# A two-layer encoder on one core: the order of layer 1's projections, norm roots in pairs, later transposes, fewer query loads

## Chip, cores and metric

The kernel runs on one core of a Trainium2 chip. The metric is the device time of one execution in microseconds (us), lower is better. Five engines take part, each with an instruction list of its own that it works off in order: TensorE (PE) multiplies matrices, VectorE (DVE), ScalarE (ACT) and GpSimd (POOL) do elementwise work, SyncE (SP) issues the DMA transfers. SBUF is the on-chip memory, PSUM the one that PE writes to.

## Reference

Sequence 2048, width 1024, fp32. Only layer 1 ("odd") is touched by the change:

```python
def odd_layer(x, norm_g, w_in, w_out, qn, kn, ..., subln_g, cos, sin, lambda_init):
    h = rms_norm(x, norm_g)
    q, k, v, gate = jnp.split(h @ w_in, [C_QK, 2 * C_QK, 2 * C_QK + C_W], axis=-1)
    q = rms_norm(q.reshape(b, s, C_HEADS, 2, HEAD_DIM), qn)      # 8 heads, two halves of 64
    k = rms_norm(k.reshape(b, s, C_HEADS, 2, HEAD_DIM), kn)
    q1, q2, k1, k2 = apply_rope(q[..., 0, :]), ...               # rotary by cos, sin
    o = differential_attention(q1, q2, k1, k2, v, lam)           # (softmax1 - lam * softmax2) @ v
    o = rms_norm(o, subln_g) * (1.0 - lambda_init)
    return x + (o.reshape(b, s, C_W) * jax.nn.silu(gate)) @ w_out
```

Layer 0 ("even") has two attention mixers and an output projection of its own, and stands before layer 1.

## The kernel before

**Tiling.** The 2048 tokens are 4 blocks of 512, a block is 4 tiles of 128. Every matrix product is made of three matmuls of 128x512, since each operand is split into a high and a low part (`wH`, `wL` for weights, `hH`, `hL` for the normed input, "hidden"): lines L214 to L216 are wH·hH, wL·hH and wH·hL. An output tile of 128 tokens by 512 columns is 8 × 3 = 24 matmuls in one PSUM place (`p1mm`, four places).

**Stages.** Names begin with the stage: `p0` layer 0's projections, `m` its mixers and its output projection (`mom`), `p1` layer 1's projections, `c` layer 1's attention with gate (`cG`) and output (`com`).

**Layer 1's projections** go over two halves of two blocks each. A half first makes hidden for its two blocks: per tile load x (`p1xt`), square and root of the mean on ACT and DVE, scale (DVE), 8 transposes of 128x128 on PE (`p1trh`), the copies `p1hH` on ACT (L336) and the rests `p1hL` on DVE (L337). Then come six groups of 512 columns: two of queries (tab "q"), two of keys (tab "k"), two of values ("cv"). A group's weights are four chunks of 512 KB (`p1ws`), split by ACT (`p1wH`, L309) and POOL (`p1wL`, L311), with two staging buffers and 28 places for split tiles, 16 to a group. For a query or key tile, ACT squares (`p1sq`, L361), DVE sums over each of 8 heads (`p1qss`, L362), `rstd` computes a root by small instructions on 128x8 (L203 to L208: `p1q8ln`, `p1q8y` on ACT, `p1q8ms`, `p1q8u` twice, `p1q8r` on DVE), DVE multiplies by it (`p1xn`, L366) and forms two half-width rotary products (`p1t`, L373), and POOL multiplies by the cosine (L377) and adds (L378). When a block's four tiles are done, PE transposes them (`p1trq`, L385), ACT copies the high part (`p1eH`), DVE the rest (`p1eL`, L391), and both are stored. `tables()` builds the rotary tables for queries and keys at the start of layer 1's projections, from `cos` and `sin`. A values tile is one ACT copy and a store.

**Ahead.** Beside these groups, the weights of attention (output weights, gate weights) are loaded, split and stored as `wgH`, `wgL` by a generator, one item of four chunks at a time.

**Attention** goes block by block; per head it loads query tiles (`cqd`, `cql`), keys `ck` and values `cv`; PE does scores (`cS`), transposes (`ctr`) and products (`cO`), and between them gate columns (`cG`) from hidden and `cwH`, `cwL` (loaded from `wgH`, `wgL`). For later blocks hidden is loaded again (`p1hH<-hH`).

**What sets the order.** A scheduler places each engine's instructions in a fixed list, from the program and its own timeline; pools are stacked in SBUF, so a tile can have to wait until an older one in the same place is released. All DMAs are issued by SP in order.

Of the kernel before, what the change touches and what calls it, by code (L numbers as in the profile page):

```python
# [10 lines left out]
F32 = mybir.dt.float32  # L11
# [7 lines left out]
P = 128  # L19
S = 2048  # L20
# [12 lines left out]
def f32(ap):  # L33
    return ap.bitcast(F32)
# [52 lines left out]
class Trunk:  # L87
# [136 lines left out]
    def _project(self, es, layer):  # L224
# [39 lines left out]
        def tables():  # L264
            if layer == 0:
                self.parameters(xp.tile([P, D], F32, tag="xt", name=n + "tmp"))
            self.cos = sb.tile([P, S // P, 32], F32, tag="xn", name=n + "cos", bufs=5)
            self.sin = sb.tile([P, S // P, 32], F32, tag="xn", name=n + "sin", bufs=5)
# [3 lines left out]
            with self.tc.issue_after(self.added) if layer else nullcontext():  # L272
                tabs["q"] = self.rope_tables(tb, self.gain[gq], 0.125 if layer else -0.125, n + "tq")
                tabs["k"] = self.rope_tables(tb, self.gain[gk], 1.0, n + "tk")

        if layer == 1:
            tables()
# [78 lines left out]
        def normed(ps, nh, tab, t):  # L356
            wd = nh * HD
            v3 = lambda ap: ap.rearrange("p (h d) -> p h d", d=HD)
            sq = sb.tile([P, 512], F32, tag="sq", name=n + "sq")
            ss = sm.tile([P, 8], F32, tag="qss", name=n + "qss")  # L360
            nc.scalar.activation(sq[:, :wd], ps[:, :wd], AF.Square)  # L361
            nc.vector.tensor_reduce(ss[:, :nh], v3(sq[:, :wd]), AX.X, ALU.add)  # L362
            r = self.rstd(sm, ss[:, :nh], nh, 1.0 / HD, n + f"q{nh}")
            xn = sb.tile([P, 512], F32, tag="xn", name=n + "xn", bufs=5)
            xv = v3(xn[:, :wd])
            nc.vector.tensor_tensor(xv, v3(ps[:, :wd]), r.unsqueeze(2).to_broadcast([P, nh, HD]), ALU.mult)  # L366
            if tab is None:
                return xn
            C, Sn = tabs[tab]
            t2 = sb.tile([P, 512], F32, tag="t2", name=n + "t2")  # L370
            tv = v3(t2[:, :wd])
            for o in (0, 32):
                nc.vector.tensor_tensor(  # L373
                    tv[:, :, o:o + 32], xv[:, :, 32 - o:64 - o],
                    Sn[:, t, o:o + 32].unsqueeze(1).to_broadcast([P, nh, 32]), ALU.mult,
                )
            nc.gpsimd.tensor_tensor(xv, xv, C[:, t, :].unsqueeze(1).to_broadcast([P, nh, HD]), ALU.mult)  # L377
            nc.gpsimd.tensor_tensor(xn[:, :wd], xn[:, :wd], t2[:, :wd], ALU.add)  # L378
            return xn
# [39 lines left out]
        ahead = later()  # L419
        for half in range(2):  # L420
            blocks = (NB - 1 - 2 * half, NB - 2 - 2 * half)
            ready = None
# [7 lines left out]
            if not tabs:  # L430
                tables()
            h.append(hidden(blocks[1], 1))
            self.last_hidden = h[1]
            for gi, (kind, c0, width, o) in enumerate(groups):
                w = ready or weights(c0, width)
                ready = None
                if gi >= self.AHEAD:
                    next(ahead, None)
                for bi, b in enumerate(blocks):
# [21 lines left out]
                    for j in range(NTB):  # L461
# [3 lines left out]
                        if kind == "qk":  # L465
                            xs.append(normed(ps, 8, o["tab"], t))
                        elif kind == "akv":
                            xs.append(normed(ps, 2, o["tab"], t))
# [12 lines left out]
                        else:  # L481
                            vt = gp.tile([P, 512], F32, tag="v", name=n + "v", bufs=3)
# [381 lines left out]
    def _mix1(self, es):  # L864
# [4 lines left out]
        sm = pool("sm", 8)  # L869
        ot = pool("ot", 4)  # L870
        yp = pool("y", 2 * KT)
        vp = pool("v", 4)
        pp = pool("pp", 20)
        kp = pool("kp", 4)
        sb = pool("sb", 2)
# [85 lines left out]
        def values(h, b, res):  # L961
# [3 lines left out]
            for kt in range(nkt):  # L965
                j0 = max(0, kt - b * NTB)
                wd = (NTB - j0) * P
                tp = ptr.tile([P, 512], F32, tag="tr", name=n + "tr")
                kk = (kt % 4) * P
                for j in range(j0, NTB):  # L970
                    nc.tensor.transpose(tp[:, (j - j0) * P:(j - j0 + 1) * P], us[j][kt // 4][:, kk:kk + P], self.ident)  # L971
                T = sb.tile([P, 512], F32, tag="pt", name=n + "pt", bufs=6)
                nc.vector.tensor_copy(T[:, :wd], tp[:, :wd])  # L973
# [297 lines left out]
```

## Time and profile before

| What | Value |
| --- | --- |
| three runs | 2804.6 us median, 2803.25 to 2808.34 |
| profiled execution | 2808.08 us, span 2806.3 us |
| mean granted PE clock of the profiled execution | 0.987 |
| PE busy | 2697.3 us (96%) |
| layer 1's projections | about 1164 to 1763 us of the span |
| attention of layer 1 | about 1763 us to the end |

The profile is of one execution. "Busy" is the time in which an engine executes, "waited" the time in which it stood until another engine or a transfer released it; the granted clock is the share of full speed that TensorE ran at. Times inside the span are us from its start.

### The profile page before, as it was taken

Reading aid. Unit: us, or ns where it says so; the run is one execution under the profiler, and the core shown is the slowest. Engines: PE = TensorE matmul, PEld = TensorE weight load, DVE = VectorE, ACT = ScalarE, POOL = GpSimd, SP = SyncE. Lnnn points to the kernel's source line nnn. Section 1 sums busy time; section 2 is a strip of 40 time slices with the busy share of each in tenths; the row PEclk is TensorE's granted clock in tenths of the full one; section 3 lists DMA queues with packets and bytes.
Section 4 is the critical chain, followed back from the end, with each engine's and each line's share of the span. In section 5 each row is a group of like instructions: output and inputs, shape, how many; then the busy total and the mean of one; then the engine's idle time right before and its main releaser. Section 6 shows DMA issues by size and latency. Waiting matters only on the chain.

```text
span 2806.3 us, 44052 instructions
## 1 busy us (share of the span) xinstructions
PE 2697.3 (96%) x13384; PEld 2169.2 (77%) x13384; DVE 1853.8 (66%) x4616; ACT 1606.4 (57%) x4039; POOL 1462.8 (52%) x1551
## 2 busy tenths in 40 slices
PE   7999999999899999899999999999999999999998
PEld 5888888888788888777788888777676777676776
DVE  7762285346777775598808870569886878777762
ACT  5443543367767675334334331578896787777761
POOL 3541252335545454267745670457676666767661
PEclk9999999999999999999999999999999999999999
DMA  5673343738866764666885444787868666454542
GB/s 174 225 242 140 109 142 122 232 109 239 240 179 191 201 192 132 209 217 207 253 256 192 135 136 142 239 256 219 238 190 230 183 212 200 132 183 144 166 146 83
DMA packets 356093, 521.69 MB, mean 186 GB/s; under 512 B 44816, under 2 KB 139792, under 8 KB 355856
## 3 DMA queue, kind: packets, MB, share of 16 engines
q1 hardware_dynamic: 355856, 518.87, 60.2%
q8 instruction: 107, 1.75, 0.3%
q14 instruction: 130, 1.06, 0.1%
HBM read 361.70 MB, written 157.02 MB: 185 GB/s over the span
## 4 chain that ended last, share of the span: by engine, by line
PE 77%; DVE 9%; DMA 6%; ACT 3%; issue 2%; POOL 2%; SPq 1%; DVEq 0%; ACTq 0%; POOLq 0%
PE cO L975 8%; PE p1mm L215 5%; PE p1mm L214 5%; PE p1mm L216 5%; PE cS L919 4%; PE cS L920 4%; PE ctr L971 4%; PE p0mm L214 4%; PE p0mm L216 4%; PE p0mm L215 4%; PE com L214 2%; PE com L215 2%; PE com L216 2%; PE cG L214 2%; PE mom L214 2%
## 5 line engine op out<-in xcount | busy, mean ns | idle before, releaser
L926 ACT ACTIVATE cP<-cS,cnm 128x512 f32<-128x512 f32 (+3 forms) x640 | 394.1, 621 | 138.4 <-DVE cnm L923 121.9
L923 DVE TENSOR_REDUCE cnm<-cS 128x1 f32<-128x512 f32 (+3 forms) x640 | 373.4, 600 | 52.2 <-PE cS L920 45.9
L959 POOL TENSOR_TENSOR cP<-cP,cP 128x512 f32<-128x512 f32 (+1 forms) x320 | 356.4, 1143 | 27.6 <-ACT cP L957 26.7
L958 POOL TENSOR_SCALAR cP<-cP,crl,cel 128x512 f32<-128x512 f32 (+3 forms) x288 | 210.7, 745 | 231.6 <-DVE crl L940 126.5
L214 PE MATMUL p1mm<-p1wH,p1hH 128*128 128x512 f32 x768 | 303.4, 396 | 5.5 <-ACT p1wH L309 5.5
L215 PE MATMUL p1mm<-p1wL,p1hH 128*128 128x512 f32 x768 | 304.4, 397 | 0.1
L216 PE MATMUL p1mm<-p1wH,p1hL 128*128 128x512 f32 x768 | 303.9, 396 | 0.0
L975 PE MATMUL cO<-cpt,cv 128*128 128x512 f32 (+3 forms) x640 | 288.0, 535 | 2.1 <-DVE cpt L973 2.1
L311 POOL TENSOR_TENSOR p0wL<-p0ws,p0wH 128x512 fp32r<-128x512 f32 (+1 forms) x124 | 149.7, 1238 | 267.3 <-ACT p0wH L309 263.3
L919 PE MATMUL cS<-ck,cqd 128*128 128x512 f32 (+3 forms) x640 | 265.3, 418 | 6.6 <-ACT cP L926 6.0
L973 DVE COPY cpt<-ctr 128x512 f32<-128x512 f32 (+1 forms) x320 | 191.0, 604 | 107.3 <-PE ctr L971 104.1
L214 PE MATMUL p0mm<-p0wH,p0hH 128*128 128x512 f32 (+1 forms) x640 | 238.5, 374 | 7.0 <-ACT p0vt L473 4.7
L216 PE MATMUL p0mm<-p0wH,p0hL 128*128 128x512 f32 (+1 forms) x640 | 238.3, 373 | 2.0 <-DVE p0hL L337 1.9
L215 PE MATMUL p0mm<-p0wL,p0hH 128*128 128x512 f32 (+1 forms) x640 | 238.4, 373 | 0.0
L311 POOL TENSOR_TENSOR p1wL<-p1ws,p1wH 128x512 fp32r<-128x512 f32 x128 | 167.2, 1327 | 124.6 <-ACT p1wH L309 118.5
L920 PE MATMUL cS<-ck,cql 128*128 128x512 f32 (+3 forms) x640 | 232.0, 367 | 0.0
L971 PEld LDWEIGHTS ctr<-ident,cP 128*128 128x128 f32 x1088 | 138.7, 142 | 115.4 <-issue 62.3
L957 ACT ACTIVATE cP<-cP,cc 128x512 f32<-128x512 f32 (+1 forms) x320 | 189.2, 651 | 18.2 <-DVE cc L943 17.7
L971 PE MATMUL ctr<-ident,cP 128*128 128x128 f32 x1088 | 177.1, 275 | 1.8 <-POOL cP L959 1.5
L214 PEld LDWEIGHTS p1mm<-p1wH,p1hH 128*128 128x128 f32 x768 | 145.8, 190 | 34.6 <-ACT p1wH L309 5.7
L215 PEld LDWEIGHTS p1mm<-p1wL,p1hH 128*128 128x128 f32 x768 | 145.6, 190 | 29.9 <-POOL p1wL L311 0.9
L216 PEld LDWEIGHTS p1mm<-p1wH,p1hL 128*128 128x128 f32 x768 | 145.8, 190 | 28.9 <-issue 0.2
(301 smaller groups left out, 7046.9 us busy)
## 6 DMA issues: line engine op xcount, KB each, us to landing
p1ws<-in_od_w_in_dram SPq DMA_DIRECT2D x56, 512.0 KB, 4.3
p0ws<-in_ev_w_in_dram SPq DMA_DIRECT2D x48, 512.0 KB, 4.2
ck<-kH SPq DMA_DIRECT2D x144, 128.0 KB, 3.4
ck<-kL SPq DMA_DIRECT2D x144, 128.0 KB, 3.5
cv<-v SPq DMA_DIRECT2D x72, 256.0 KB, 4.0
cqd<-qH SPq DMA_DIRECT2D x128, 128.0 KB, 4.6
cql<-qL SPq DMA_DIRECT2D x128, 128.0 KB, 4.7
cwH<-wgH SPq DMA_DIRECT2D x64, 256.0 KB, 5.1
```

Of the source, the lines that this page charges most:

```text
L214: mm(ps, aH, bH, start=first, stop=False)
L215: mm(ps, aH, bL, start=False, stop=False)
L216: mm(ps, aL, bH, start=False, stop=last)
L311: low.tensor_tensor(l[:, :width], ws[:, k, :width], f32(h[:, :width]), ALU.subtract)
L919: mm(ps, qd[:, m, js], kt[:, :wd], start=True, stop=False)
L920: self.anchor = mm(ps, ql[:, m, js], kt[:, :wd], start=False, stop=True).ins
L923: nc.vector.tensor_reduce(nm[:, m, z:z + 1], ps, AX.X, ALU.max, negate=True)
L926: exp = nc.scalar.activation(chunks[z][:, :wd], ps, AF.Exp, bias=nm[:, m, z:z + 1], accum_out=acc).ins
L958: nc.gpsimd.tensor_scalar(p1, p1, rl[:, 0:1], e1, ALU.mult, ALU.mult)
L959: nc.gpsimd.tensor_tensor(p1, p1, p2, ALU.add)
L971: nc.tensor.transpose(tp[:, (j - j0) * P:(j - j0 + 1) * P], us[j][kt // 4][:, kk:kk + P], self.ident)
L975: mm(O[:, j0 * P:], v, T[:, :wd], start=(kt == 0), stop=(kt == nkt - 1), skip_group_check=True)
```

## The change

1. Group order in each half of layer 1: one values group, both query and both key groups, the other values group. The rotary tables are built after the first values group.
2. The root is computed for two tiles at once (128x16 instead of 128x8), and for the second tile of each pair the last addition is done by DVE instead of POOL.
3. A block's query and key transposes are put off until the second tile of the next block's work. There are 8 `xn` places instead of 5.
4. In half 0 the block made first lies in the pool `hv`, the second in `ev` (before, the reverse); half 1 takes its two blocks in the other order, and its last group turns once more.
5. The stack order of the pools `sb`, `g`, `w` of the projections and of most pools of attention is new.
6. Items of "ahead": before one in each of groups 2 to 5 of half 0; now two in group 5 of half 0, one in group 0 and one in group 5 of half 1.
7. Query loads of attention: 4 of 256 KB instead of 8 of 128 KB per head and block.

```diff
@@ pools of the projections
-            wp = pool("w", 28)
-            gp = pool("g", 2)
-        sb = pool("sb", 2)
+        sb = pool("sb", 2)
+        if layer == 1:
+            gp = pool("g", 3)
+            wp = pool("w", 28)
...
-            pl, tag = (self.big, "w") if layer == 0 else (self.hv, "h") if i else (ev, "v")
+            pl, tag = (self.big, "w") if layer == 0 else (ev, "v") if i else (self.hv, "h")
@@ groups
-            groups += [("cv", 2048 + 512 * i, 512, dict(c0=512 * i)) for i in range(2)]
+            values = [("cv", 2048 + 512 * i, 512, dict(c0=512 * i)) for i in range(2)]
+            groups = values[:1] + groups + values[1:]
@@ roots and rotary products
+        def squares(ps, nh, to):
...
+            nc.scalar.activation(sq[:, :nh * HD], ps[:, :nh * HD], AF.Square)
+            nc.vector.tensor_reduce(to, v3(sq[:, :nh * HD]), AX.X, ALU.add)
+
+        def normed(pss, ss, nh, tab, ts, xs):
+            wd, n2 = nh * HD, nh * len(pss)
+            r = self.rstd(sm, ss[:, :n2], n2, 1.0 / HD, n + f"q{nh}")
+            for i, ps in enumerate(pss):
...
+                    nc.gpsimd.tensor_tensor(xv, xv, C[:, ts[i], :].unsqueeze(1).to_broadcast([P, nh, HD]), ALU.mult)
+                    adds = nc.vector if layer and i else nc.gpsimd
+                    adds.tensor_tensor(xn[:, :wd], xn[:, :wd], t2[:, :wd], ALU.add)
+                xs.append(xn)
@@ loop over halves, groups, blocks, tiles
+            if layer == 1 and half == 1:
+                blocks = blocks[::-1]
...
-                if gi >= self.AHEAD:
+                for _ in range(gi >= self.AHEAD if layer == 0 else {0: half, 5: 2 - half}.get(gi, 0)):
                     next(ahead, None)
...
                         ps = project_tile(h[bi], j, w, width)
+                        if j == 1:
+                            turn()
...
                     if xs:
-                        pairs_out(xs, 4 if kind == "qk" else 1, b, o)
+                        turned.append((xs, 4 if kind == "qk" else 1, b, o))
...
+                if not tabs:
+                    tables()
+            turn()
@@ attention
-            for m in range(2):
-                r = slice(m * HD, (m + 1) * HD)
-                for part, q in (("qH", qd), ("qL", ql)):
-                    nc.sync.dma_start(f32(q[0:HD, m, :]), s[part][h, r, tok])
-                    nc.sync.dma_start(f32(q[HD:P, m, :]), s[part][h, r, tok])
+            for part, q in (("qH", qd), ("qL", ql)):
+                both = s[part][h, :, tok].rearrange("(m r) t -> r m t", m=2)
+                for o in range(2):
+                    nc.sync.dma_start(f32(q[o * HD:(o + 1) * HD]), both)
```

How this moves instructions, at three places. First, ACT's list where layer 0's output projection ends and layer 1's projections begin, before (`p1xss`, `p1xln`, `p1xy` belong to hidden's norm; `xN` at a row's end means N in a row):

```order
L336 ACTIVATE p1hH<-p1trh 128x4x128 x4
L325 ACTIVATE p1junk,p1xss<-p1xt 128x1024
L309 ACTIVATE p1wH<-p1ws 128x512
L203 ACTIVATE p1xln<-p1xss,eps 128x1
L309 ACTIVATE p1wH<-p1ws 128x512
```

and the same place after:

```order
L203 ACTIVATE p1xln<-p1xss,eps 128x1
L307 ACTIVATE p1wH<-p1ws 128x512
L204 ACTIVATE p1xy_14352<-p1xln 128x1
L307 ACTIVATE p1wH<-p1ws 128x512 x13
L334 ACTIVATE p1hH<-p1trh 128x4x128 x5
```

The first weights' high parts moved from behind four of hidden's copies to the place ahead of them, fourteen at once.

Second, DVE's list in a query or key group, where one tile follows another, before:

```order
L362 TENSOR_REDUCE p1qss<-p1sq 128x8
L205 TENSOR_SCALAR p1q8ms<-p1qss 128x8
L206 SCALAR_TENSOR_TENSOR p1q8u<-p1q8y_15179 128x8
L207 TENSOR_TENSOR p1q8u<-p1q8u,p1q8ms 128x8
L208 SCALAR_TENSOR_TENSOR p1q8r<-p1q8u,p1q8y_15179 128x8
L366 TENSOR_TENSOR p1xn<-p1mm,p1q8r 128x512
L373 TENSOR_TENSOR p1t_15191<-p1xn,p1tqS 128x8x32
L391 TENSOR_TENSOR p1eL<-p1trq,p1eH 128x512
```

and after:

```order
L205 TENSOR_SCALAR p1q8ms<-p1qss 128x16
L206 SCALAR_TENSOR_TENSOR p1q8u<-p1q8y_15914 128x16
L207 TENSOR_TENSOR p1q8u<-p1q8u,p1q8ms 128x16
L208 SCALAR_TENSOR_TENSOR p1q8r<-p1q8u,p1q8y_15914 128x16
L369 TENSOR_TENSOR p1xn<-p1mm,p1q8r 128x512 x2
L375 TENSOR_TENSOR p1t_15926<-p1xn,p1tkS 128x8x32 x2
L375 TENSOR_TENSOR p1t_15933<-p1xn,p1tkS 128x8x32 x2
L359 TENSOR_REDUCE p1qss<-p1sq 128x8
L381 TENSOR_TENSOR p1xn<-p1xn,p1t_15933 128x512
L359 TENSOR_REDUCE p1qss<-p1sq 128x8
```

One root of 128x16 stands for two of 128x8, and the second tile's addition (L381) now stands on DVE, between the next pair's reductions. POOL's list at such a place, after, with the weights' low parts (L309) between the multiplications (L379) and the first tiles' additions (L381):

```order
L379 TENSOR_TENSOR p1xn<-p1xn,p1tqC 128x512 x2
L381 TENSOR_TENSOR p1xn<-p1xn,p1t_15140 128x512
L309 TENSOR_TENSOR p1wL<-p1ws,p1wH 128x512 x6
L379 TENSOR_TENSOR p1xn<-p1xn,p1tqC 128x512 x2
L309 TENSOR_TENSOR p1wL<-p1ws,p1wH 128x512 x2
L381 TENSOR_TENSOR p1xn<-p1xn,p1t_15222 128x512
```

The multiplications now come in twos, with six of the weights' low parts ahead of one of these.

Third, SP's list in attention's second block, where hidden is loaded again (`hL`, `hH`) and gate weights (`wgH`, `wgL`) are fetched, before:

```order
L1083 DMA p1hL<-hL 128x512
L1082 DMA p1hH<-hH 128x512 x2
L1083 DMA p1hL<-hL 128x512
L894 DMA cql<-qL 64x512
L1082 DMA p1hH<-hH 128x512
L1083 DMA p1hL<-hL 128x512
L1076 DMA cwH<-wgH 128x512
L1076 DMA cwL<-wgL 128x512
```

and after:

```order
L1073 DMA ck_22717<-kL 64x512
L1116 DMA g_75<-cgt 128x512
L1103 DMA cwH<-wgH 128x512
L1103 DMA cwL<-wgL 128x512
L1110 DMA p1hL<-hL 128x512
L1109 DMA p1hH<-hH 128x512
L1018 DMA cgg<-g_75 128x512
```

The gate weights' loads moved from behind hidden's loads to the place ahead of them.

More of the change, by code (lines that the diff above doesn't have):

```diff
@@ L266, in tables @@
                 self.parameters(xp.tile([P, D], F32, tag="xt", name=n + "tmp"))
-            self.cos = sb.tile([P, S // P, 32], F32, tag="xn", name=n + "cos", bufs=5)
-            self.sin = sb.tile([P, S // P, 32], F32, tag="xn", name=n + "sin", bufs=5)
+            self.cos = sb.tile([P, S // P, 32], F32, tag="xn", name=n + "cos", bufs=5 + 3 * layer)
+            self.sin = sb.tile([P, S // P, 32], F32, tag="xn", name=n + "sin", bufs=5 + 3 * layer)
             nc.sync.dma_start(self.cos, a["cos"].rearrange("(t p) d -> p t d", p=P))
@@ L271, in tables @@
             gq, gk = ("ev_a_q_norm", "ev_a_k_norm") if layer == 0 else ("od_q_norm", "od_k_norm")
[L272 to L277, printed above, removed]
+            tabs["q"] = self.rope_tables(tb, self.gain[gq], 0.125 if layer else -0.125, n + "tq")
+            tabs["k"] = self.rope_tables(tb, self.gain[gk], 1.0, n + "tk")
         if layer == 0:
@@ L354, in project_tile @@
             return ps
-        def normed(ps, nh, tab, t):
-            wd = nh * HD
-            v3 = lambda ap: ap.rearrange("p (h d) -> p h d", d=HD)
+        v3 = lambda ap: ap.rearrange("p (h d) -> p h d", d=HD)
+        def squares(ps, nh, to):
             sq = sb.tile([P, 512], F32, tag="sq", name=n + "sq")
[L360 to L379, printed above, removed]
@@ L419, in _project, with turn @@
         ahead = later()
+        turned = []
+        def turn():
+            while turned:
+                pairs_out(*turned.pop(0))
         for half in range(2):
             blocks = (NB - 1 - 2 * half, NB - 2 - 2 * half)
+            if layer == 1 and half == 1:
+                blocks = blocks[::-1]
             ready = None
@@ L429, in _project @@
                 h = [hidden(blocks[0], 0)]
-            if not tabs:
+            if layer == 0 and not tabs:
                 tables()
             h.append(hidden(blocks[1], 1))
-            self.last_hidden = h[1]
+            self.last_hidden = h[0]
             for gi, (kind, c0, width, o) in enumerate(groups):
@@ L436, in _project @@
                 ready = None
-                if gi >= self.AHEAD:
+                for _ in range(gi >= self.AHEAD if layer == 0 else {0: half, 5: 2 - half}.get(gi, 0)):
                     next(ahead, None)
-                for bi, b in enumerate(blocks):
+                turns = list(enumerate(blocks))
+                if layer == 1 and half == 1 and gi == len(groups) - 1:
+                    turns.reverse()
+                for bi, b in turns:
                     if kind == "gate":
@@ L464, in _project @@
                         ps = project_tile(h[bi], j, w, width)
[L465 to L468, printed above, removed]
+                        if j == 1:
+                            turn()
+                        if kind in ("qk", "akv"):
+                            nh, i = 8 if kind == "qk" else 2, j % 2 if layer else 0
+                            if i == 0:
+                                pss, ss = [], sm.tile([P, 16], F32, tag="qss", name=n + "qss")
+                            pss.append(ps)
+                            squares(ps, nh, ss[:, i * nh:(i + 1) * nh])
+                            if i == layer:
+                                normed(pss, ss, nh, o["tab"], (t - i, t), xs)
+                        if kind == "akv":
                             vt = sb.tile([P, 2, 192], F32R, tag="sq", name=n + "vt")
@@ L480, in _project @@
                             nc.sync.dma_start(s["bv"][tok, :], f32(vt).rearrange("p a e d -> p (a e d)"))
-                        else:
-                            vt = gp.tile([P, 512], F32, tag="v", name=n + "v", bufs=3)
+                        elif kind == "cv":
+                            vt = gp.tile([P, 512], F32, tag="v", name=n + "v")
                             nc.scalar.activation(vt, ps, AF.Copy)
@@ L485, in _project @@
                     if xs:
-                        pairs_out(xs, 4 if kind == "qk" else 1, b, o)
+                        turned.append((xs, 4 if kind == "qk" else 1, b, o))
+                        if layer == 0:
+                            turn()
+                if not tabs:
+                    tables()
+            turn()
     def out_tile(self, y, w, j, t, c, xin, xout, sb, pmm, n, tag, xtag="xr", xbufs=None, order=range(KT), after=None):
@@ L869, in _mix1 @@
         sm = pool("sm", 8)
+        pp = pool("pp", 20)
         ot = pool("ot", 4)
+        vp = pool("v", 4)
         yp = pool("y", 2 * KT)
-        vp = pool("v", 4)
-        pp = pool("pp", 20)
+        tp = pool("pt", 6)
+        sb = pool("sb", 2)
         kp = pool("kp", 4)
-        sb = pool("sb", 2)
         NS, NTR, NO, NM = self.BANKS1
```

21 lines of the change are left out of this document (17 added, 4 removed).

## The prediction

> **What bounds the kernel now.** I began with the page's busy times.
>
> ```profile
> PE 2697.3 (96%) x13384; PEld 2169.2 (77%) x13384; DVE 1853.8 (66%) x4616; ACT 1606.4 (57%) x4039; POOL 1462.8 (52%) x1551
> span 2806.3 us, 44052 instructions
> ```
>
> TensorE is the bound, and the change takes no matmul away (it adds and removes none on PE). So it can only win back PE's idle time and time at a lowered clock, or add to them. Next I cut the span into stages. The columns are length, then busy time of PE, PEld, DVE, ACT, POOL, then the granted clock, the DMA share and GB/s.
>
> ```profile
> 1162.00:1234.00 72.00, 62.61 (x295) 50.98 (x295) 66.84 (x122) 37.00 (x88) 37.46 (x29) 0.93 0.70 246
> 1234.00:1300.00 66.00, 63.23 (x293) 51.96 (x292) 56.05 (x95) 22.62 (x54) 45.55 (x37) 0.97 0.53 182
> 1300.00:1371.00 71.00, 65.74 (x292) 51.73 (x291) 66.98 (x95) 28.52 (x65) 55.75 (x44) 0.95 0.75 245
> 1371.00:1763.00 392.00, 391.59 (x1835) 324.96 (x1833) 203.00 (x383) 133.96 (x294) 192.67 (x148) 1.00 0.57 180
> 1763.00:2806.30 1043.30, 1009.74 (x4583) 745.21 (x4583) 755.18 (x1942) 745.42 (x1948) 663.25 (x704) 0.98 0.62 187
> ```
>
> Layer 1's projections run from 1162 to 1763. I count a stage's loss as idle time plus (1 − clock) × length: 9.4 + 5.0 = 14.4 us to 1234, 2.8 + 2.0 = 4.8 to 1300, 5.3 + 3.6 = 8.8 to 1371, and 0.4 over the whole rest. The first three hold 28.0 us, while DVE is busy 85 to 94% of them. What PE waited for there, and after it in the attention (total, times, longest):
>
> ```profile
> PE p1trq L385 <- DVE p1eL L391: 7.2, 3, 2.9
> PE p1mm L214 <- ACT p1wH L309: 5.5, 1, 5.5
> PE p1trh L332 <- DVE p1q8u L206: 3.5, 1, 3.5
> ...
> PE cG L214 <- DMA cwH<-wgH: 10.9, 4, 4.7
> PE cS L919 <- ACT cP L926: 6.0, 9, 1.6
> ```
>
> Then short windows around single gaps, since a gap costs more than itself:
>
> ```profile
> 1165.00:1177.00 12.00, 6.93 (x29) 5.25 (x30) 12.00 (x21) 6.83 (x15) 5.71 (x5) 0.72 0.38 114
> 1206.00:1215.00 9.00, 5.53 (x25) 4.63 (x24) 8.83 (x18) 3.04 (x12) 5.63 (x5) 0.81 0.40 132
> 1234.00:1246.00 12.00, 9.23 (x38) 7.23 (x37) 10.45 (x16) 3.74 (x10) 9.47 (x9) 0.86 0.40 130
> 1126.00:1136.00 10.00, 7.68 (x34) 6.03 (x33) 5.93 (x17) 4.83 (x12) 0.00 (x0) 1.00 1.05 264
> 1970.00:1981.00 11.00, 6.26 (x25) 5.01 (x24) 4.01 (x13) 5.65 (x15) 3.00 (x5) 0.69 1.05 351
> 2132.00:2143.00 11.00, 6.53 (x20) 4.48 (x19) 2.82 (x6) 3.93 (x10) 5.18 (x6) 0.69 0.89 265
> ```
>
> Idle time of 2.3 us (1126) left the clock at 1.00; 2.8 us (1234) brought it to 0.86 and 3.5 us (1206) to 0.81, which is 1.7 us more in each (12 × 0.14, 9 × 0.19). Wins here therefore come as a gap plus 1.7 to 3.4 us. The Trainium skill, "TensorE: Matmul & The Clock Gate", section "Why this matters for your kernels", advises against idle gaps over about 3 us because one such window halves the clock. The trace agrees in kind, but its 2.8 us gap already paid. By the page's limit the third window would lose 2.8 us and no clock, and the sum below would be 1.7 us smaller.
>
> **Part 1: first weights, hidden first, tables later.** Before, ACT's order puts the first weights' copy behind hidden rows, in places that layer 0 still held; PE stood for it 5.5 us, and at 1165 lost 5.1 + 12 × 0.28 = 8.4 us. After, 14 copies stand ahead of the first hidden tile, in places free earlier, under layer 0's last output tiles, where PE has work. What is late next is hidden itself: 16 transposes and the DVE subtractions behind them. I leave 2 us, so −6.4. The two windows at 1206 and 1234 lost 3.5 + 1.7 and 2.8 + 1.7 = 9.7 us while DVE was busy 8.8 of 9 and 10.5 of 12 us: tables, roots and hidden compete there. After, the values' blocks need only an ACT copy, and DVE has hidden alone; the tables are built beside the values' second block. Cos and sin now load behind layer 0's last stores, so the tables can be late for the first query group: I leave 4 us of the 9.7. Of the remaining 1.1 us (19.2 − 8.4 − 9.7) I leave all. Together −12.1; bounds −19 (nothing left) and 0 (a table or hidden wait as long as today's).
>
> **Part 2: roots for two tiles, and the moved add.** These are DVE's and POOL's groups of the projections (busy, mean ns, idle before), and the root's durations as minimum/median/maximum:
>
> ```profile
> L207 DVE TENSOR_TENSOR p1q8u<-p1q8u,p1q8ms 128x8 f32<-128x8 f32 x64 | 47.2, 738 | 1.7
> L366 DVE TENSOR_TENSOR p1xn<-p1mm,p1q8r 128x512 f32<-128x512 f32 x64 | 44.2, 691 | 2.6
> L362 DVE TENSOR_REDUCE p1qss<-p1sq 128x8 f32<-128x512 f32 x64 | 43.4, 678 | 7.2 <-ACT p1sq L361 6.6
> L391 DVE TENSOR_TENSOR p1eL<-p1trq,p1eH 128x512 fp32r<-128x512 f32 x64 | 41.5, 683 | 38.4 <-ACT p1eH L390 23.3 <-DMA kL<-p1eL 14.4 <-DMA qL<-p1eL 0.7
> L205 DVE TENSOR_SCALAR p1q8ms<-p1qss 128x8 f32<-128x8 f32 x64 | 39.1, 611 | 2.0
> L373 DVE TENSOR_TENSOR p1t<-p1xn,p1tqS 128x256 f32<-128x256 f32 x64 | 36.1, 604 | 3.1 <-DVE p1xn L366 0.5
> L208 DVE SCALAR_TENSOR_TENSOR p1q8r<-p1q8u,p1q8y 128x8 f32<-128x8 f32 x64 | 32.6, 509 | 2.0
> L206 DVE SCALAR_TENSOR_TENSOR p1q8u<-p1q8y 128x8 f32<-128x8 f32 x64 | 25.5, 399 | 12.8 <-ACT p1q8y L204 12.5
> ...
> L311 POOL TENSOR_TENSOR p1wL<-p1ws,p1wH 128x512 fp32r<-128x512 f32 x128 | 167.2, 1327 | 124.6 <-ACT p1wH L309 118.5 <-DMA wgH<-p1wH 4.1 <-DMA wgL<-p1wL 1.6
> L378 POOL TENSOR_TENSOR p1xn<-p1xn,p1t 128x512 f32<-128x512 f32 x64 | 83.5, 1305 | 2.9
> ...
> L207 DVE TENSOR_TENSOR p1q8u<-p1q8u,p1q8ms x64: 153/1182/1270, 1192.3 to 1673.6; 128x8 f32<-128x8 f32 x64
> ```
>
> A root is 0.611 + 0.399 + 0.738 + 0.509 = 2.257 us; 32 fewer are 72 us of DVE, and 64 small ACT operations go too. A tile costs DVE 0.678 + 2.257 + 0.691 + 2 × 0.604 + 0.683 = 5.5 us, a pair 11.0. PE needs for a pair 48 matmuls and 8 transposes at 392.00/1835 = 0.214, 12.0 us. So DVE fills 92% and loses PE wherever it also has something else. After, a pair costs 11.0 − 2.26 + 0.69 (the add that comes over from POOL, priced as L366, the nearest 128x512 DVE operation) = 9.5 us, 79%. Together with the transposes' delay by a block or two, which gives the last tile's chain room, I let the 8.8 us of 1300–1371 fall to 1.8: −7.0 (bounds −8.8 and 0). From 1371 on there is 0.4 us to win, so the relief is worth nothing there.
>
> The added wait: DVE's add of each second tile waits for POOL's multiplication. Behind it on DVE stand the next pair's reduction and the subtractions that free the projection's PSUM places, and PE waits for these. In a pair POOL has two multiplications, one add and four wL on average: 3 × 1.305 + 4 × 1.327 = 9.2 us of 12.0, but its order has six wL in a row ahead of one of the multiplications. I take +2, bounds 0 and +24 (rival 1).
>
> L207 has two SBUF inputs and 128x8 elements, and takes 0.15 or 1.18 us; POOL is busy 52 to 79% of the first three stages. Doubled width will not make it longer than that. The added DVE operation also has two SBUF inputs; if it is held as L207 is, it takes 0.69 + 1.0 = 1.7 us, a pair 10.5 us, still under 12.0: no cost to PE, less slack. The Trainium skill, "SBUF — State Buffer", section "Who interferes with whom", says that DVE's two-input SBUF operations and POOL share a port pair under an exclusive lock, so one waits out the other; L207's two values agree, and the rule speaks against moving an add from POOL to DVE while POOL works. By it the sum moves by nothing as long as DVE keeps its 1.5 us per pair.
>
> **Part 3: weights at the half's turn.** Half 0 now ends with a values group, and the two output-weight items of 4 chunks each are split there, with the chunks that half 1 needs first behind them. PE's order there goes chunk by chunk over four tiles, that is, it expects to wait.
>
> ```profile
> p1ws<-in_od_w_in_dram SPq DMA_DIRECT2D x16, 512.0 KB, 5.0
> 1386.00:1460.00 74.00, 74.00 (x334) 61.27 (x333) 11.29 (x18) 25.57 (x48) 44.51 (x36) 1.00 0.94 291
> ```
>
> Before, 16 such chunks took 74 us, 4.6 each, with DMA at 94%. Twelve need 55 us; PE has the values group (192 × 0.214 = 41), hidden's 32 transposes (7) and some 5 us of early start, 53. I take +3 (bounds 0 and +10, at 5.2 us a chunk).
>
> **Part 4: attention.** The same bytes go in half as many query loads. cwH at 1968.5 was issued behind a whole reload of hidden:
>
> ```profile
> L1076 SPq DMA_DIRECT2D cwH<-wgH x4: 319/352/431, 1968.5 to 1991.4; - x4
> 1957.00:1967.00 10.00, 10.00 (x46) 7.03 (x45) 8.90 (x25) 8.41 (x25) 5.72 (x6) 1.00 1.02 272
> ```
>
> DMA ran at 1.02 just before, so it is bytes queued ahead that made it late. After, SP issues this cwH and its cwL ahead of the reload: of 8.1 us (4.7 idle + 11 × 0.31 of clock, window 1970) I win 6. The next one (2132, 7.9 us) comes only one pair of loads earlier: −2. Bounds −16 and 0. The other pools' places shift no PE order that I could price: 0, covered by DVE at 755 and ACT at 745 of 1043 us. Layer 0 keeps its order: 0. Half 1 and the last values group: 0, the cover being a clock of 1.00 and 0.4 us lost in 392; if it is gone, the price is rival 2's.
>
> **Sum.** −12.1 − 7.0 + 2 + 3 − 8 = −22.1. The profiled execution took 2808.1 us (span 2806.3), so 2786.0; the runs' median, 2804.6, lies 3.5 under it, so **2782.5**.
>
> **Rivals.**
> 1. *DVE held behind POOL, slower* (0.09). The six wL in a row are 8.0 us. Four PSUM places hold the projection's tiles, so PE can do two more tiles (48 × 0.214 = 10.3 us) before it needs one of the pair that DVE is at; reduction, root and multiplication of that pair take 3.6, which leaves 6.7, and I say 5 with ACT's square ahead of them. Then each of the eight query and key groups (four in each half) stands 3 us, plus 1.7 of clock: +38 in place of the +2, 2782.5 + 36 = 2818. It decides from (22.1 + 2)/8 = 3.0 us a group, clock included. For it: POOL's fixed order and the new wait. Against: 12.0 − 9.5 = 2.5 us of slack per pair on DVE, and xn places for eight tiles instead of five.
> 2. *The weights chain at the turn decides* (0.07): DMA is slower with stores beside it. 12c − 53 us; it cancels the −25.1 of the rest at c = 6.5 us a chunk. At 5.9 it is +18: 2797, at 6.5 no change, 2805. Against: the 4.6 above holds with 94% DMA share and stores in it.
> 3. *Attention gains nothing* (0.17), because the late cwH is DMA bytes and those stay: 2782.5 + 8 = 2790.5.
> 4. *All three stalls vanish* (0.12): −19 − 8.8 − 16 = −44: about 2764 with +3 for the turn.
>
> **Chances.** My forecast, within 7 us, gets 0.55. Rival 1 lies mostly over 2804.6, rival 2 mostly under. Faster or slower by under 0.2% (5.6 us), about what a measurement here can tell, counts as the same. That gives faster 0.85, same 0.06, slower 0.09. The range runs from rival 4 to rival 2's middle, 2764 to 2799.
>
> **What would show it.** Right: no wait of p1mm for p1wH near the stage's start; clock 1.00 in 1180–1370; half as many small root operations; DVE under 85% in the query and key groups; one cwH wait under 2 us and the other near 3. Wrong: PE waiting for DVE operations that themselves waited on POOL's xn, PE waiting for p1wH in the middle of the stage, a table wait in the first query group, or a cwH wait of the old length.

## The result and the profile after

The changed kernel takes 2823.4 us (median of 4 runs, 2818.68 to 2825.4) against 2803.93 us before: 1.0064 times as long by the runs' means, 95% interval 1.0046 to 1.0081. Forecast was 2782.5, a gain. Its profiled execution took 2824.8 us, with a span of 2822.8 us.

Where the time lies is read from the first and last start of three kinds of matmul. In a tile's view of the trace the columns are duration in ns (minimum/median/maximum), then first and last start. First the kernel before:

```profile
L216 PE MATMUL mom<-mw,myL x256: 387/392/628, 745.4 to 1163.9; 128*128 128x512 f32 x128
L216 PE MATMUL p1mm<-p1wH,p1hL x768: 387/389/774, 1173.0 to 1757.4; 128*128 128x512 f32 x192
```

and the changed one:

```profile
L216 PE MATMUL mom<-mw,myL x256: 387/392/628, 747.0 to 1165.2; 128*128 128x512 f32 x128
L216 PE MATMUL p1mm<-p1wH,p1hL x768: 387/389/775, 1168.0 to 1742.2; 128*128 128x512 f32 x192
```

From layer 0's last matmul to the projections' last, 593.5 us have become 577.0: 16.5 less. From there to the span's end, 1048.9 (2806.3 − 1757.4) have become 1080.6 (2822.8 − 1742.2): 31.7 more. Layer 0, whose order did not change, ended 1.3 later. −16.5 + 31.7 + 1.3 = +16.5, the difference of the spans. So the projections won 16.5 of a forecast 14.1, and attention, forecast to win 8, lost 31.7. The stages of the changed kernel, with the columns of the prediction's windows:

```profile
1165.30:1300.00 134.70, 134.70 (x652) 112.70 (x651) 87.76 (x163) 52.30 (x111) 45.55 (x34) 1.00 0.54 180
1300.00:1371.00 71.00, 71.00 (x335) 59.19 (x335) 57.34 (x88) 24.43 (x49) 45.08 (x34) 1.00 0.43 138
1371.00:1742.50 371.50, 364.11 (x1707) 302.32 (x1706) 215.45 (x342) 130.45 (x261) 190.00 (x143) 0.99 0.64 205
1742.50:1790.00 47.50, 31.13 (x122) 23.56 (x121) 15.78 (x56) 17.12 (x51) 11.59 (x16) 0.78 0.72 201
1790.00:2822.80 1032.80, 991.57 (x4489) 727.58 (x4487) 747.29 (x1897) 730.33 (x1902) 652.36 (x689) 0.98 0.64 185
```

The first two rows show PE busy throughout at full clock: the 28 us that the prediction found there are gone. The third row has 7.4 us idle and some 3.4 of clock where the kernel before had 0.4 in all. The fourth row is the loss's largest piece: in attention's first 47.5 us PE is idle for 16.4 and the granted clock falls to 0.78, another 10.5, together 26.9. The kernel before lost 0.6 us in as long a stretch from the same point, and did nearly twice the work in it (226 PE instructions against 122):

```profile
1757.60:1805.00 47.40, 46.80 (x226) 38.27 (x225) 25.53 (x98) 31.46 (x91) 22.95 (x30) 1.00 0.76 235
```

What PE, and behind it ACT, waited for in the changed kernel from 1740 to 1790 (total, times, longest), and the issue of the last values stores:

```profile
PE cS L946 <- ACT cP L953: 13.0, 2, 9.0
PE cG L214 <- DMA cwH<-wgH: 2.7, 1, 2.7
...
ACT cP L953 <- DMA v<-p1v: 15.9, 1, 15.9
ACT p1v L505 <- DMA v<-p1v: 5.6, 1, 5.6
ACT csg L1024 <- DMA cgg<-g: 5.5, 1, 5.5
...
L506 SPq DMA_DIRECT2D v<-p1v x2: 325/358/392, 1753.5 to 1755.7; - x2
```

PE waits for scores' exponentials (cP), and ACT cannot write one of these until the last store of values has read the place under it. That store is issued at 1755.7, 13.5 us after the projections' last matmul started: SP issues in a fixed order, and 14 other transfers were issued between that tile's copy (1743.5) and its store. Here are the last 42 us of the projections, after and then before:

```profile
1700.00:1742.00 42.00, 42.00 (x195) 34.95 (x194) 9.70 (x14) 9.26 (x17) 13.87 (x11) 1.00 0.97 263
...
1715.00:1757.00 42.00, 42.00 (x187) 34.77 (x186) 0.00 (x0) 4.20 (x7) 0.00 (x0) 1.00 0.48 127
```

DMA is at 97% where it was at 48%. Before, two groups of values stood there, whose only traffic was their stores and attention's first loads. Now the last keys' stores and an item of weights (load, split, store) fall into the same 42 us beside these.

Later in attention the waits for cwH are shorter than before (10.9 us in all, 4.7 the longest), and waits for query loads are new (from 1790 on):

```profile
PE cS L946 <- ACT cP L953: 7.5, 9, 2.3
PE cS L947 <- DMA cql<-qL: 6.5, 2, 4.3
PE ctr L998 <- ACT csq L1031: 4.9, 1, 4.9
PE cG L214 <- DMA cwH<-wgH: 4.8, 3, 1.8
```

### The profile page after: what moved, and what is told of

It is laid out like the page before. It is cut to its first block, busy times and chain, and to the rows that moved or that the text cites. A ratio compares the mean times of both kernels' runs of the same rounds, so it can differ in the third digit from the quotient of the medians.

```text
span 2822.8 us, 43687 instructions
## 1 busy us (share of the span) xinstructions
PE 2700.3 (96%) x13384; PEld 2172.0 (77%) x13384; DVE 1832.4 (65%) x4520; ACT 1599.0 (57%) x3975; POOL 1431.2 (51%) x1519
## 4 chain that ended last, share of the span: by engine, by line
PE 75%; DMA 12%; DVE 5%; ACT 3%; issue 2%; POOL 2%; SPq 2%; DVEq 0%; ACTq 0%; POOLq 0%
PE cO L1002 8%; PE p1mm L214 5%; PE p1mm L216 5%; PE p1mm L215 5%; PE cS L946 4%; PE cS L947 4%; PE ctr L998 4%; PE p0mm L214 3%; PE p0mm L216 3%; PE p0mm L215 3%; PE com L214 2%; PE com L215 2%; PE com L216 2%; PE mom L214 2%; PE mom L215 2%
## 5 line engine op out<-in xcount | busy, mean ns | idle before, releaser
L309 POOL TENSOR_TENSOR p0wL<-p0ws,p0wH 128x512 fp32r<-128x512 f32 (+1 forms) x124 | 149.4, 1232 | 266.3 <-ACT p0wH L307 263.8
L309 POOL TENSOR_TENSOR p1wL<-p1ws,p1wH 128x512 fp32r<-128x512 f32 x128 | 174.2, 1385 | 151.9 <-ACT p1wH L307 143.6
```

What stands on the lines that cost most here:

```text
L309: low.tensor_tensor(l[:, :width], ws[:, k, :width], f32(h[:, :width]), ALU.subtract)
```

## The experiments

All comparisons are ratios to the kernel before, run beside it on the same chip; its median there was 2809 to 2812 us. "Projections" is the trace's length from layer 0's last matmul to the projections' last, "attention" from there to the span's end. These two come from one execution of each kernel, and single executions scatter: e6's profiled one is its slowest of six, 4.6 us over its median. Where a length and a ratio differ by a few us, the ratio decides.

### First: which of attention's edits, or the jam before it

e1 swaps two pools in the changed kernel:

```diff
-        sm = pool("sm", 8)
         pp = pool("pp", 20)
+        sm = pool("sm", 8)
```

> The changed kernel with two pools of attention swapped in their stack: the probabilities' places (pp) come before the small tiles (sm). Every engine's list stays the same; only addresses move by 2.25 KB, so that no probability tile lies over a values tile of the projections any more. Theory A (the place: ACT's second probability tile waits for the last values store, 15.9 us, and PE behind it 9.0 and 4.1 us plus a lowered clock): about 2808 us, 15 us less than the changed kernel's 2823, and PE's wait for cP at the start of attention gone or under 3 us. Theory B (the DMA queue is jammed at the end of the projections, and whoever waits for it next is as late): 2818 or more, with the wait moved to cwH, cgg or cv. Theory C (merged query loads): no difference, 2823.

e2 gives attention's pools the order of before (the copies `cpt` go back into `sb`):

```diff
-        pp = pool("pp", 20)
         ot = pool("ot", 4)
-        vp = pool("v", 4)
         yp = pool("y", 2 * KT)
-        tp = pool("pt", 6)
-        sb = pool("sb", 2)
+        vp = pool("v", 4)
+        pp = pool("pp", 20)
         kp = pool("kp", 4)
+        sb = pool("sb", 2)
```

> The changed kernel with attention's pools in the order of before (scores' outputs, gate outputs, values and probabilities where they were), query loads still merged. Theory A: as the swap or better, 2800 to 2810, since the first probability tiles lie over split weights again. Theory B: 2815 or more. Theory C: 2823.

e3 puts the eight query loads of before back in place of the four.

> The changed kernel with eight query loads of 128 KB per head and block instead of four of 256 KB. Theory A: the start of attention as in the changed kernel (PE waits 13 us for cP), only block two's waits for cql (6.5 us) may go: 2815 to 2823. Theory C (the merged loads land later and cost most of the 32 us): under 2805.

e4 moves one item of attention's weights:

```diff
-{0: half, 5: 2 - half}.get(gi, 0)
+{0: half, 2: half, 5: 2 - 2 * half}.get(gi, 0)
```

> The changed kernel with half 1's last item of attention's weights split in its third group instead of its last one. The item is 4 chunks of 512 KB loaded and stored, 4 MB in the last 43 us. Theory B (the jam): the last values store lands about 10 us earlier, 2808 to 2813. Theory A: the wait for the values store shrinks by what the store comes earlier, at most some 6 us of time; with SP's order little changed, 2817 to 2823.

| kernel | ratio to before (95%) | projections | attention |
| --- | --- | --- | --- |
| before | 1 | 593.5 | 1048.9 |
| changed | 1.0064 (1.0046 to 1.0081) | 577.0 | 1080.6 |
| e1 pools swapped | 1.0060 (1.0038 to 1.0083) | 577.9 | 1086.3 |
| e2 old places | 1.0013 (0.9993 to 1.0033) | 576.5 | 1069.6 |
| e3 old query loads | 0.9980 (0.9965 to 0.9995) | 579.2 | 1064.1 |
| e4 item earlier | 1.0010 (0.9995 to 1.0025) | 582.0 | 1061.7 |

e1 won nothing: the wait moved, it did not go. In its trace DVE waits for the same store:

```profile
DVE cnm L950 <- DMA v<-p1v: 16.0, 1, 16.0
```

The small tiles had come to lie over the values' place, so e1 did not test the place. e2, e3 and e4 each win 0.5 to 0.8% by three different edits, and theory C's did best. Their gains in attention, 11.0, 16.5 and 18.9 us, add up to 46.4, more than the 31.7 lost, so they overlap and no one of them is the whole cause. e4's item costs some 5 us in the projections, where it now stands.

### Second: each alone

e5 puts the last thing that attention writes over the values tiles, and is meant to leave the engines' lists as they are:

```diff
         ld = pool("ld", 2)
-        sm = pool("sm", 8)
         pp = pool("pp", 20)
+        yp = pool("y", 2 * KT)
         ot = pool("ot", 4)
         vp = pool("v", 4)
-        yp = pool("y", 2 * KT)
         tp = pool("pt", 6)
         sb = pool("sb", 2)
         kp = pool("kp", 4)
+        sm = pool("sm", 8)
```

> The changed kernel with attention's pools stacked so that what lies over the projections' values tiles is the last thing attention writes (the heads' results, cy), and the small tiles lie over x's places. The lists of PE, DVE, ACT, POOL and SP stay as in the changed kernel. After the first four runs: in the swapped version the wait for the last values store only went over to DVE's small tile cnm, which had come to lie over the same place, so the place was not taken out of play there. Theory A (the place): without any early tile over it the start of attention wins 10 to 18 us: 0 to 8 us above the kernel before on the same chip (the changed kernel is 18 above). Theory B (the jammed DMA queue): the next transfer (cwH, cgg, cv) is as late, 14 or more above the kernel before.

e6 is the changed projections with all of attention as before.

> The changed projections with the whole attention of before (its pools' order and its eight query loads). If the projections' 16.5 us are kept and the loss comes from attention's two edits alone: 12 to 17 us under the kernel before. If the order of the groups (values last, key stores and an item of weights in the last 43 us) costs by itself: within 6 us of the kernel before, with PE waiting at the start of attention for ck, cwH or a place under a values store.

e7 is the kernel before with only the query loads changed:

```diff
-            for m in range(2):
-                r = slice(m * HD, (m + 1) * HD)
-                for part, q in (("qH", qd), ("qL", ql)):
-                    nc.sync.dma_start(f32(q[0:HD, m, :]), s[part][h, r, tok])
-                    nc.sync.dma_start(f32(q[HD:P, m, :]), s[part][h, r, tok])
+            for part, q in (("qH", qd), ("qL", ql)):
+                both = s[part][h, :, tok].rearrange("(m r) t -> r m t", m=2)
+                for o in range(2):
+                    nc.sync.dma_start(f32(q[o * HD:(o + 1) * HD]), both)
```

> The kernel before with the merged query loads alone. Theory C (a 256 KB load into 64 partitions takes the DMA queue 1.24 us where two of 128 KB take 0.99): 128 x 0.25 = 32 us more queue time, of which only the parts where DMA is full reach PE: 4 to 12 us slower than before. Rival (same bytes, fewer issues: nothing): within 3 us of before.

e8 is the changed kernel with the edits of e3, e4 and e5 together.

> The changed kernel with the heads' results over the values tiles, the old query loads, and half 1's last weights item in the third group. If place, query loads and the item add up (A, B and C each true in part): 12 to 18 us under the kernel before, PE's waits at the start of attention under 4 us. If they overlap and something else holds the start: 0 to 6 under.

| kernel | ratio to before (95%) | projections | attention |
| --- | --- | --- | --- |
| e5 results over values | 1.0043 (1.0026 to 1.0059) | 577.3 | 1079.7 |
| e6 old attention | 0.9967 (0.9955 to 0.9979) | 577.0 | 1062.5 |
| e7 before, merged loads | 1.0071 (1.0055 to 1.0086) | 594.7 | 1067.5 |
| e8 all three | 0.9951 (0.9935 to 0.9968) | 582.2 | 1047.1 |

e7 decides: the merged loads alone make the kernel before 0.71% slower, 20 us, as much as the whole change. My expectation for it, 4 to 12 us, was too low. e5, 12 us over the kernel before, lies between theory A's 0 to 8 and theory B's 14 or more. ACT's wait for the values store is gone from it and its first 47.5 us of attention lose 13.3 instead of 26.9, but attention as a whole is only 0.9 shorter: while the merged loads stay, what the start wins is lost again later. e6, 9 us under the kernel before, also lies between its two expectations. It keeps the projections' gain but pays 13.6 us in attention without any edit of attention, nearly all of them in the first 47.5 us (8.1 idle, 5.2 of clock). Its PE waits there for keys:

```profile
PE cS L946 <- DMA ck<-kH: 6.5, 1, 6.5
```

So the new order of the projections, with what it puts into their last 42 us, costs by itself. e8 has neither the merged loads nor that item of weights at the end: attention is as short as before, the start of attention is full,

```profile
1744.00:1792.00 48.00, 48.00 (x234) 39.82 (x233) 26.37 (x100) 32.16 (x92) 24.04 (x31) 1.00 0.81 248
```

and the kernel beats both others, by its ratio 14 us under before.

### Third: why the merged loads cost, and which parts of the projections count

All of these are e8 with one edit. e9 puts the merged loads back. e10 loads 256 KB too, but into 128 rows. In e10 and e18 a tile's lower and upper 64 rows hold the two halves of a head instead of one half twice, so they time the loads and are no finished kernel:

```diff
+            for part, q in (("qH", qd), ("qL", ql)):
+                for m in range(2):
+                    nc.sync.dma_start(f32(q[:, m, :]), s[part][h, :, tok])
```

> The best version so far (e8) with the merged query loads put back: four of 256 KB, each into 64 partitions of 2 x 512. In the runs so far these loads alone cost 20 us in the kernel before. Expected: 8 to 20 us above e8, that is 7 us under to 5 us above the kernel before; landings of queries 1.2 us apart in a full queue.

> As e9, but each 256 KB load goes into all 128 partitions of one half-column (128 x 512), so count and bytes are the same as in e9. The queries are in part the wrong ones: a tile's lower and upper 64 rows hold the two different halves of a head instead of one half twice; loads, matmuls and all other work are the same. Theory P (the rate of a load goes by the partitions it reaches): landings of queries about 0.65 us apart like those of cwH (256 KB into 128 partitions), and the time of e8 or a little under it, 12 to 18 us under the kernel before. Theory L (fewer and larger loads hold the eight lanes longer, whatever they reach): as e9.

e17 keeps eight loads of 128 KB with `for part` as the outer loop and `for m` as the inner one; e18 is e10 with `for m` as the outer loop.

> e8 with the same eight query loads of 128 KB in another order: high parts of both halves, then low parts. A head's first scores read the high and the low part of half 0 over all 128 rows: four of eight loads in e8, six of eight here, all four in the merged form (e9), three of four in e10. Theory O (the merged loads cost because the first scores have to wait for more of the bytes): between e8 and e9, 4 to 14 us above e8. Theory P (because a large load into 64 rows is slow): as e8 within 3 us.

> e10 with the order of its four loads changed: both parts of half 0 first, so that the first scores need two of four loads, as many bytes as in e8. As in e10 a tile's rows are in part of the wrong half. Theory O: 3 to 8 us under e10, at or under e8's time (0.9951 of the kernel before). Theory P alone: as e10 (0.9953).

| kernel | ratio to before (95%) | attention |
| --- | --- | --- |
| e8: eight loads of 128 KB, 64 rows | 0.9951 (0.9935 to 0.9968) | 1047.1 |
| e9: four of 256 KB, 64 rows | 1.0016 (1.0002 to 1.0030) | 1065.8 |
| e10: four of 256 KB, 128 rows | 0.9953 (0.9929 to 0.9977) | 1055.0 |
| e17: eight, high parts first | 0.9944 (0.9922 to 0.9966) | 1048.1 |
| e18: four, 128 rows, by half | 0.9938 (0.9920 to 0.9957) | 1047.5 |

e9 repeats e7 on another base, 0.65% or 18 us. With 128 rows per load the time is back, so theory L falls and P holds by the times. Against theory O stands e17: six of eight loads before the first scores cost nothing (forecast 4 to 14 us over e8). e18 can't tell, since its 4 us under e10 are what O foretold and lie within the noise, so O may still be a small part. P also foretold landings 0.65 us apart, and that failed: the low parts (`cql`) land a median 7.3 us after their issue in e10, 7.5 in e9 and 4.8 in e8. DMA's engine time fits the times better than the landings do. For 1763 to 2640 us of e8, e9, e10 and e18, in this order, the rows give packets, MB and the share of the 16 engines:

```profile
q1 hardware_dynamic: 122140, 172.65, 66.7%
...
q1 hardware_dynamic: 118384, 169.88, 68.1%
...
q1 hardware_dynamic: 118745, 170.54, 66.3%
...
q1 hardware_dynamic: 120044, 172.23, 67.1%
```

Share by MB is 0.386, 0.401, 0.389 and 0.390: the merged 64-row form takes 4% more of DMA's time for the same bytes, 0.04 × 0.667 × 877 = 23 us over the window, the 128-row forms 1%. Over this window all runs with eight loads have 0.381 to 0.389 and all with the merged 64-row form 0.397 to 0.406, with one exception: e3 has eight loads and 0.395, and yet is 0.84% faster than the changed kernel (0.397). So the measure goes with the loads' form in all runs but one, and that engine time is how they cost is likely, not shown. Why 64-row loads of 128 KB, which alternate between the halves every 128 KB, don't pay this is open; loads of 128 KB into the same half in a row were not tried.

Then the projections. e11 puts the moved addition back on POOL, e12 the transposes right after their block, e13 takes one root for each tile (with all additions on POOL), e14 the old order of groups, e15 the old stack order of `w`, `g`, `sb`, e16 the edits of e11 and e12 together.

> e8 with the last addition of every query and key tile on POOL, as before, and the roots still for two tiles at once. If the moved addition is hidden, as the prediction had it: within 3 us of e8. If DVE's wait for POOL costs: 3 us or more under e8. If POOL becomes late without it (3 x 1.3 + 1.3 + 4 x 1.33 = 10.5 us of 12.0 a pair): 3 to 10 us above e8.

> e8 with the query and key transposes of layer 1 right after their block, as before. If the delay is what took PE's waits for the last tile's chain away: PE waits at every block's end for DVE's or POOL's xn, 16 blocks by 1 to 3 us, 10 to 40 us above e8 before the scheduler fills some of it; if the roots for two tiles alone did it: within 4 us of e8.

> e8 with one root for each tile and all last additions on POOL, everything else as in e8. If the roots in pairs carry the projections' gain as the prediction's part 2 has it (DVE 92% to 79% of a pair's time): 7 us or more above e8, with PE waiting for DVE's xn or eL in the query and key groups. If the order of the groups and the places carry it: within 3 us of e8.

> e8 with the groups in the order of before (queries, keys, values) and the tables built after the first hidden block. If the early stalls go because DVE has hidden alone beside the first values group (part 1): 5 to 12 us above e8 with waits of PE for DVE between 1160 and 1300. In exchange the end of the projections is relieved of key stores, which costs nothing in e8 (PE waits under 0.2 us there): no gain there.

> e8 with the projections' pools stacked as before (split weights first, then values, then the rest). Part 1's first term: the first weights wait again for places of layer 0 until its last matmul; PE loses 5 us and a lowered clock at the start, 6 to 10 us above e8. If the first weights now hide behind the hidden transposes: within 3 us.

> e8 without the later transposes and without the moved addition, which e11 and e12 showed singly to bring nothing that can be told (0.9932 and 0.9928 of the kernel before, against 0.9951 of e8, intervals overlapping). If both are idle: 14 to 20 us under the kernel before. If the one covers for the other: 3 us or more above e8.

| kernel | ratio to before (95%) | projections |
| --- | --- | --- |
| e8 | 0.9951 (0.9935 to 0.9968) | 582.2 |
| e11 addition on POOL | 0.9932 (0.9912 to 0.9951) | 580.1 |
| e12 transposes at once | 0.9928 (0.9903 to 0.9953) | 580.7 |
| e13 root per tile | 0.9956 (0.9943 to 0.9969) | 582.0 |
| e14 queries first | 0.9935 (0.9907 to 0.9962) | 581.2 |
| e15 split weights first in the stack | 0.9980 (0.9964 to 0.9995) | 590.7 |
| e16 e11 and e12 | 0.9941 (0.9921 to 0.9961) | 583.3 |

Only e15 stands apart: 8 us, all in the projections. The stage 1162 to 1300 of e15, then of e8:

```profile
1162.00:1300.00 138.00, 130.80 (x604) 107.83 (x603) 74.51 (x134) 53.94 (x111) 62.44 (x48) 0.98 0.54 189
...
1162.00:1300.00 138.00, 138.00 (x667) 115.44 (x666) 90.93 (x169) 53.00 (x113) 46.17 (x35) 1.00 0.56 185
```

7.2 us idle and 2.8 of clock against nothing. Undone singly, the other edits (groups, roots, delay, moved addition) are worth nothing that four to ten runs can tell, and e8 without two of them is as fast. So the expectation for e14, 5 to 12 us over e8, failed, and that for e13, 7 us or more if the paired roots carry the gain, did not come. No version among e8, e11, e12, e13, e14 and e16 can be told from another. Two items of the change were undone in none of these: the blocks' places and turns (4), and the move of attention's weights out of half 0's middle (6).

## Why the prediction was wrong, step by step

**Part 1, first weights and hidden** (−12.1). The direction was right and the size 7 us short: 19.2 us of loss became none, the bound that the prediction gave. Its first term (first weights in places that come free earlier, −6.4) is worth 8.5 us in e15's trace (590.7 − 582.2). The path is confirmed in part only: ACT does stand 14.9 us there until layer 0's last matmul, but at hidden's copies, and of the 7.2 us idle PE waits 4.5 for hidden and 2.7 for weights. The reason for the other half, values first so that DVE has hidden alone, failed. With queries first (e14) DVE is busy 89% of the same stage, and PE loses 0.9 us there:

```profile
1162.00:1300.00 138.00, 137.13 (x674) 114.10 (x673) 122.90 (x218) 56.22 (x123) 61.23 (x46) 1.00 0.58 189
```

What took the other half away is open. A rival that no run undid is item 6: before, eight chunks of output weights were loaded between 1248 and 1343, beside the stages that lost; after, the first is loaded at 1370.6.

**Part 2, roots in pairs** (−7.0). The 8.8 us went, 7.0 of them as forecast, but not for the reason given. The step that failed is "DVE fills 92% and loses PE wherever it also has something else". In e13, with one root per tile, DVE fills the same share and PE loses nothing:

```profile
1300.00:1371.00 71.00, 71.00 (x339) 59.25 (x338) 65.30 (x102) 26.95 (x64) 50.26 (x40) 1.00 0.39 125
```

65.3 of 71 is 92%. Whether the delayed transposes are what covers it there was not tried (both edits undone together), nor item 6, with which DMA's share of this stage fell from 0.75 to 0.43. That the time came out near is luck as far as the roots go. The moved addition was sized right:

```profile
L381 DVE TENSOR_TENSOR p1xn<-p1xn,p1t 128x512 f32<-128x512 f32 x32 | 53.9, 1684 | 31.8 <-POOL p1xn L379 31.8
```

It took a mean of 1.68 us against my 1.7, its shortest 0.68. The Trainium skill's rule in "SBUF — State Buffer", "Who interferes with whom", by which a DVE operation with two SBUF inputs contends with POOL for a port, points the same way. That POOL held it is argued, not shown. DVE stood 31.8 us for POOL, and without that (e11) the kernel is not faster by more than the noise: rival 1 did not occur.

**Part 3, the half's turn** (+3). The stage from 1371 on lost 7.4 us idle and 3.4 of clock (0.72 from 1448 to 1460). PE's own waits name hidden rather than weights:

```profile
PE p1mm L214 <- ACT p1hH L334: 3.5, 1, 3.5
PE p1mm L214 <- DVE p1xn L369: 2.7, 1, 2.7
PE p1trh L330 <- DVE p1hL L335: 0.6, 1, 0.6
PE p1mm L214 <- ACT p1wH L307: 0.6, 1, 0.6
```

But hidden was late because ACT, whose list is in order, stood 6.0 us for a chunk of weights ahead of it:

```profile
1451.42 1.15 ACT L307 ACTIVATE p1wH<-p1ws 128x512 fp32r<-128x512 f32 x2 [5.98 <-DMA p1ws<-in_od_w_in_dram]
1452.48 0.58 ACT L505 ACTIVATE p1v<-p1mm 128x512 f32<-128x512 f32 x1
1452.95 2.05 ACT L334 ACTIVATE p1hH<-p1trh 128x512 fp32r<-128x512 f32 x4
```

PE's transposes had ended at 1450.1. So the mechanism was right, late weights at the turn, and the path is one that the term left out, through ACT: 3.5 us idle and 3.4 of clock. Rival 2 occurred in part, at a lower price than its +18. The 2.7 us stand at 1532, where a query group begins and PE waits for DVE to free a PSUM place; e13, with one root for each tile, has 3.0 there, so the pairs are not the cause. The term was about 8 us too small.

**Part 4, attention** (−8). This is where the sign turned. The step that failed is "The same bytes go in half as many query loads", for which I set no price. The measured price is 18 to 20 us (e7; e9 against e8), and 24 us undone in the changed kernel (e3). I had a row that should have warned me: the window 1957 had DMA at 1.02 with 272 GB/s where 1970 had 1.05 with 351; a full queue whose rate depends on what goes through it means that a load's shape can be a cost. The rest is 12 to 14 us by subtraction. It failed at "Half 1 and the last values group: 0": e6, with none of attention's edits, pays 13.6. The last 42 us, which I held for covered because PE lost nothing there, were to take the last keys' stores and an item of weights as well. "The other pools' places shift no PE order that I could price: 0" overlooked that an order that stays can still wait for a place, and the start shows it (15.9 us of ACT, 13.0 of PE). What the places cost by themselves stays open: with the merged loads e2 wins 11.0 us of attention and e5 0.9 (14 and 6 us of time), and without them e3 and e6, which differ in the places, are 1.6 apart. The cwH term had the right direction (10.9 us of waits became 2.7 + 4.8), but queries took over what it freed.

**Sum.** Projections −14.1 forecast (with Parts 1 to 3), −16.5 measured; attention −8 forecast, +31.7 measured. That the projections come within 2.4 us is in part luck: Parts 1 and 2 with the added wait were forecast at −17.1, and 28 us went, while Part 3 was some 8 us too small. Rivals 3 and 4 varied attention's gain, between none and 16 us, and none had attention lose.

The clock again made small waits dear: of the first 47.5 us of attention, 16.4 were idle and 10.5 went to the clock. A single gap of 2.7 us ending at 1532 left the clock at 1.00 (1526 to 1538), where the prediction's gap of 2.8 us had gone with 0.86.

## What to carry to other kernels

Price a merged transfer by a measurement of its own form, not by bytes and count, above all where the queue is full. Here four loads of 256 KB into 64 rows lost 18 to 20 us, and four into 128 rows neither lost nor won anything that can be told. When a reorder moves stores to the end of a stage, look at what the next stage's first tiles lie over and at how full the DMA queue is in the last microseconds, not only at whether PE is busy there. Undo edits singly before believing in them: of five edits in the projections that were undone, only the stack order of three pools gave a part that could be pinned down, 8 of 16.5 us.

## What was not expected of the hardware

Four loads of 256 KB into 64 rows went with 3 to 4% more DMA engine time per MB of attention's traffic than eight of 128 KB into 64 rows or four of 256 KB into 128 rows (0.401 against 0.386 and 0.389, window 1763 to 2640), and with 18 to 20 us of kernel time. The Trainium skill, "SBUF — State Buffer", "Door 1: The DMA port swizzle", says that 64 rows reach only half of SBUF's ports, 196 against 328 GB/s at 1 MiB; e9 against e10 agrees in direction. By the same rule the eight loads of 128 KB into 64 rows should be as dear, and e8 shows that they are not.

The small root operations became shorter although wider. In the prediction's row L207 had a median of 1182 ns; here it is

```profile
L207 DVE TENSOR_TENSOR p1q8u<-p1q8u,p1q8ms x32: 166/176/1218, 1230.1 to 1700.3; 128x16 f32<-128x16 f32 x32
```

176 ns, and its mean went from 738 to 464. e11 and e13 both have all additions on POOL and differ from each other in the pairs alone: with pairs (e11) the median is 177, and with one root for each tile

```profile
L207 DVE TENSOR_TENSOR p1q8u<-p1q8u,p1q8ms x64: 152/1218/1278, 1222.5 to 1701.4; 128x8 f32<-128x8 f32 x64
```

it is 1218 again. So it comes with the pairs, and neither with the addition's place nor with the order of the groups. Why is open.
